# Softmax over a 32768-wide vocabulary: other column pieces for the middle tiles and the last tile

## Chip, cores, metric

One core of one Trainium2 chip. The metric is the time of one execution on the device, in microseconds. The span of a profile is about 1.8 us shorter than the time of the same execution.

## The reference

```python
batch, seq, vocab = 16, 256, 32768          # float32, standard normal draws, temperature 1.0

def reference(logits, temperature):
    scaled = logits / temperature
    scaled = scaled - scaled.max(axis=-1, keepdims=True)
    exp_scaled = np.exp(scaled)
    return (exp_scaled / exp_scaled.sum(axis=-1, keepdims=True)).astype(np.float32)
```

4096 rows of 128 KB are read once and written once: 537 MB each way.

## The kernel before

Each row is cut into two halves on two partitions, so a tile is 128 half-rows of 16384 columns (8.4 MB, 64 KB per partition), and there are 64 tiles in three buffers. Per tile: one load, per column piece a max (DVE) and an exp with that piece's own max (ACT, which also sums), a small chain of statistics that joins pieces and halves, then a scaling shared by DVE and ACT, then one store. A load is issued when the store that last used its buffer has landed.

```python
_SPLIT = 2
_BUFS = 3
_LOAD = 16384
_PIECES = (4096, 4096, 4096, 2048, 2048)     # columns of a piece
_ON_DVE = (4096, 4096, 2048, 0, 0)           # of these, scaled by DVE; ACT scales the rest
_END = 4096                                  # pieces of the first and the last tile
_END_ON_DVE = 2560
# ...
    def store(t, a, b):
        engine = nc.sync if t >= G - 2 else nc.scalar     # SP for the last two tiles, else ACT
        engine.dma_start(out=o[t * P : (t + 1) * P, a:b], in_=buf[t % _BUFS][:, a:b])
# ...
    def normalise(t):
        # ... sizes, on_dve and at: the pieces of this tile
        for k in range(K):
            xc = xs[:, at[k] : at[k] + sizes[k]]
            nc.vector.tensor_reduce(out=nm[:, k : k + 1], in_=xc, axis=X, op=A.max, negate=True)
            # ... (a step for other temperatures, not run here)
            nc.scalar.activation(out=xc, in_=xc, func=Exp, bias=nm[:, k : k + 1],
                                 scale=inv_t, accum_out=ssum[:, k : k + 1])
            if t == 1 and k == 0:
                store(0, 0, W)
        # ... statistics: f[:, k] is the factor of piece k
        for k in range(K):
            a, b, c = at[k], at[k] + on_dve[k], at[k] + sizes[k]
            if b > a:
                nc.vector.tensor_scalar_mul(out=xs[:, a:b], in0=xs[:, a:b], scalar1=f[:, k : k + 1])
            if c > b:
                nc.scalar.activation(out=xs[:, b:c], in_=xs[:, b:c], func=Copy, scale=f[:, k : k + 1])
            if t == G - 1:
                store(t, a, c)               # the last tile is stored piece by piece
        if 0 < t < G - 1:
            store(t, 0, W)

    with tc.manual_schedule():
        for t in range(_BUFS):
            load(t)
        for t in range(G):
            normalise(t)
            if t and t + _BUFS - 1 < G:
                load(t + _BUFS - 1)
```

Of the kernel before, what the change touches and what calls it, by code (L numbers as in the profile page):

```python
# [1 line left out]

# [4 lines left out]


_SPLIT = 2
_BUFS = 3  # L10
_LOAD = 16384
_PIECES = (4096, 4096, 4096, 2048, 2048)
_ON_DVE = (4096, 4096, 2048, 0, 0)
_END = 4096
_END_ON_DVE = 2560
_SETS = 3


@with_exitstack
def kernel(  # L20
    ctx: ExitStack,
    tc: tile.TileContext,
    logits: bass.AP,
    temperature: bass.AP,
    out: bass.AP,
):
    nc = tc.nc
    inv_t = 1.0 / float(temperature)
    P = nc.NUM_PARTITIONS
    fp32 = mybir.dt.float32  # L30
    Exp = mybir.ActivationFunctionType.Exp
    Copy = mybir.ActivationFunctionType.Copy
    X = mybir.AxisListType.X
    A = mybir.AluOpType

    xf = logits.flatten_outer_dims()
    of = out.flatten_outer_dims()
    N, V = xf.shape
    W = V // _SPLIT
    assert sum(_PIECES) == W and len(_PIECES) == len(_ON_DVE)  # L40
    x = xf.rearrange("n (h v) -> (n h) v", h=_SPLIT)
    o = of.rearrange("n (h v) -> (n h) v", h=_SPLIT)
    G = N * _SPLIT // P
    assert G * P == N * _SPLIT
    n_rounds = _SPLIT.bit_length() - 1
    K = max(len(_PIECES), W // _END)

    pool = ctx.enter_context(tc.tile_pool(name="fixed", bufs=1))
    buf = [pool.tile([P, W], fp32, tag=f"x{b}", name=f"x{b}") for b in range(_BUFS)]
    widths = dict(nm=K, ssum=K, ee=K, f=K, ttj=K, nMh=2, Sh=2, rS=1)  # L50
    stat = [
        {
            k: pool.tile([P, w], fp32, tag=f"{k}{s}", name=f"{k}{s}")
            for k, w in widths.items()
        }
        for s in range(_SETS)
    ]

    def load(t: int) -> None:
        n = _END if t in (0, G - 1) else _LOAD  # L60
        for s in range(0, W, n):
            nc.sync.dma_start(  # L62
                out=buf[t % _BUFS][:, s : s + n],
                in_=x[t * P : (t + 1) * P, s : s + n],
            )

    def store(t: int, a: int, b: int) -> None:

        engine = nc.sync if t >= G - 2 else nc.scalar
        engine.dma_start(  # L70
            out=o[t * P : (t + 1) * P, a:b], in_=buf[t % _BUFS][:, a:b]
        )

    def combine(v, op) -> None:
        for j in range(n_rounds):
            mask = [i ^ (1 << j) for i in range(32)]
            nc.vector.stream_shuffle(  # L77
                out=v[:, j + 1 : j + 2], in_=v[:, j : j + 1], mask=mask
            )
            nc.vector.tensor_tensor(  # L80
                out=v[:, j + 1 : j + 2],
                in0=v[:, j : j + 1],
                in1=v[:, j + 1 : j + 2],
                op=op,
            )

    def normalise(t: int) -> None:
        xs = buf[t % _BUFS]
        if t in (0, G - 1):
            sizes = [_END] * (W // _END)  # L90
            on_dve = [_END_ON_DVE] * len(sizes)
        else:
            sizes, on_dve = _PIECES, _ON_DVE
        K = len(sizes)
        at = [sum(sizes[:k]) for k in range(K)]
        st = stat[t % _SETS]
        nm, ssum, ee, f, ttj = (st[k][:, :K] for k in ("nm", "ssum", "ee", "f", "ttj"))
        nMh, Sh, rS = st["nMh"], st["Sh"], st["rS"]
        for k in range(K):
            xc = xs[:, at[k] : at[k] + sizes[k]]  # L100
            nc.vector.tensor_reduce(  # L101
                out=nm[:, k : k + 1], in_=xc, axis=X, op=A.max, negate=True
            )
            if inv_t != 1.0:
                nc.vector.tensor_scalar_mul(
                    out=nm[:, k : k + 1], in0=nm[:, k : k + 1], scalar1=inv_t
                )
            nc.scalar.activation(  # L108
                out=xc,
                in_=xc,  # L110
                func=Exp,
                bias=nm[:, k : k + 1],
                scale=inv_t,
                accum_out=ssum[:, k : k + 1],
            )
            if t == 1 and k == 0:

                store(0, 0, W)
        nc.vector.tensor_reduce(out=nMh[:, 0:1], in_=nm, axis=X, op=A.min)  # L119
        combine(nMh, A.min)  # L120
        nc.scalar.activation(  # L121
            out=ee, in_=nm, func=Exp, bias=nMh[:, n_rounds : n_rounds + 1], scale=-1.0
        )
        nc.vector.tensor_tensor_reduce(  # L124
            out=ttj,
            in0=ee,
            in1=ssum,
            scale=1.0,
            scalar=0.0,
            op0=A.mult,  # L130
            op1=A.add,
            accum_out=Sh[:, 0:1],
        )
        combine(Sh, A.add)
        nc.vector.reciprocal(out=rS, in_=Sh[:, n_rounds : n_rounds + 1])  # L135
        nc.vector.tensor_scalar_mul(out=f, in0=ee, scalar1=rS)  # L136
# [3 lines that stand above are left out]
                nc.vector.tensor_scalar_mul(  # L140
                    out=xs[:, a:b], in0=xs[:, a:b], scalar1=f[:, k : k + 1]
                )
            if c > b:
                nc.scalar.activation(  # L144
                    out=xs[:, b:c], in_=xs[:, b:c], func=Copy, scale=f[:, k : k + 1]
                )
            if t == G - 1:
                store(t, a, c)
# [12 lines that stand above are left out]
# [1 line left out]
_INS = ['logits', 'temperature']  # L162
_OUTS = [((16, 256, 32768), 'float32')]

_NUMBERS = {'temperature': 1.0}


# [26 lines left out]
```

## Time and profile before

| | before |
|---|---|
| time, median of 3 executions | 2496.47 us (2496.07 to 2497.04) |
| span of the profile | 2496.7 us |
| DVE busy, ACT busy | 1575.6 us, 1367.8 us |
| HBM traffic | 430 GB/s over the span |
| DVE waiting for loads | 683.8 us, 66 times |

The page gives busy time per engine, the busy share of 40 equal slices in tenths, and the DMA queues with the share of sixteen DMA engines' span that their packets took. The waits say who waited for whom: total, times, longest. The prediction quotes the lines. To be kept in mind for later: the page counts a DMA engine as busy for the whole duration of a packet, and equal packets do not all take the same time (64 KB took 2418 to 4252 ns in this profile).

### The profile page before, as it was taken

The page shows a single profiled execution, that of the slowest core. Times are in us where ns is not written, and L with a number is a line of the kernel's source. Part 1 is how long each engine was busy: PE and PEld are TensorE (multiplying, and loading weights), DVE is VectorE, ACT ScalarE, POOL GpSimd, SP SyncE. Part 2 cuts the span into 40 slices and gives each one's busy share as a digit, 9 for nine tenths or more (in the row PEclk, how much of TensorE's full clock was granted, in tenths as well). Part 3 has the DMA queues.
Part 4 walks back from the last instruction along what each step waited for, and adds up shares of the span by engine and source line. Part 5 has one row for each costly group of instructions (what it writes and reads, how often), then busy time and mean ns, then how long its engine had stood idle before and what let it go on. Part 6 is the DMA issues. An engine that isn't in the chain of part 4 may idle for free.

```text
span 2496.7 us, 2616 instructions
## 1 busy us (share of the span) xinstructions
DVE 1575.6 (63%) x1216; ACT 1367.8 (55%) x895; POOL 0.2 (0%) x4
## 2 busy tenths in 40 slices
DVE  6576665766657656576565665656657566565665
ACT  6464654645546455464554645546455464554655
POOL 0000000000000000000000000000000000000000
DMA  9999999999999999999999999999999999999998
GB/s 419 436 429 430 433 437 436 435 437 426 434 434 437 433 426 435 434 436 423 433 433 433 435 425 436 436 433 425 435 422 436 421 437 436 421 436 422 436 429 380
DMA packets 19748, 1073.91 MB, mean 430 GB/s; under 512 B 2192, under 2 KB 2192, under 8 KB 2192
## 3 DMA queue, kind: packets, MB, share of 16 engines
q1 hardware_dynamic: 10800, 553.65, 51.4%
q10 hardware_dynamic: 8928, 520.10, 48.4%
q14 instruction: 20, 0.16, 0.0%
HBM read 536.87 MB, written 536.87 MB: 430 GB/s over the span
## 4 chain that ended last, share of the span: by engine, by line
DMA 73%; DVE 16%; ACT 9%; another core or an unknown queue 2%; issue 0%; SPq 0%; DVEq 0%; ACTq 0%
DMA x<-in_logits_dram 37%; DMA out_dram<-x 36%; DVE nm L101 12%; ACT x L108 7%; DVE x L140 3%; ACT x L144 2%; DVE f L136 0%; ACT ee L121 0%; DVE rS L135 0%; DVE Sh L80 0%; DVE ttj L124 0%; DVE Sh L77 0%; SPq L62 0%; DVEq L189 0%
## 5 line engine op out<-in xcount | busy, mean ns | idle before, releaser
L101 DVE TENSOR_REDUCE nm<-x 128x1 f32<-128x4096 f32 x318 | 1117.5, 3579 | 683.8 <-DMA x<-in_logits_dram 683.8
L108 ACT ACTIVATE x<-x,nm 128x4096 f32<-128x4096 f32 x318 | 965.4, 3036 | 1025.3 <-DVE nm L101 1025.3
L144 ACT ACTIVATE x<-x,f 128x2048 f32<-128x2048 f32 (+1 forms) x194 | 370.9, 1975 | 74.0 <-DVE f L136 74.0
L140 DVE TENSOR_SCALAR x<-x,f 128x4096 f32<-128x4096 f32 (+2 forms) x194 | 372.2, 1975 | 2.5 <-DVE f L136 0.2
L124 DVE CUSTOM_DVE_ANT_0 ttj<-ee,ssum 128x5 f32<-128x5 f32 (+1 forms) x64 | 10.6, 166 | 196.7 <-ACT ee L121 196.7
L108 ACT ACTIVATION_READ_ACCUMULATOR x<-x,nm 128x1 f32 x318 | 59.2, 186 | 0.0
L121 ACT ACTIVATE ee<-nm,nMh 128x5 f32<-128x5 f32 (+1 forms) x64 | 18.1, 284 | 0.0
L136 DVE TENSOR_SCALAR f<-ee,rS 128x5 f32<-128x5 f32 (+1 forms) x64 | 14.8, 231 | 2.2
L135 DVE RECIPROCAL rS<-Sh 128x1 f32<-128x1 f32 x64 | 10.5, 164 | 2.2
L80 DVE TENSOR_TENSOR Sh<-Sh 128x1 f32<-128x1 f32 x64 | 10.2, 159 | 2.2
L80 DVE TENSOR_TENSOR nMh<-nMh 128x1 f32<-128x1 f32 x64 | 10.2, 159 | 2.2
L119 DVE TENSOR_REDUCE nMh<-nm 128x1 f32<-128x5 f32 (+1 forms) x64 | 10.1, 158 | 2.2
L77 DVE STREAM_SHUFFLE Sh<-Sh 128x1 f32<-128x1 f32 x64 | 9.7, 151 | 0.0
L77 DVE STREAM_SHUFFLE nMh<-nMh 128x1 f32<-128x1 f32 x64 | 9.7, 151 | 0.0
L108 ACT ACT_TABLE_LOAD x1 | 1.3, 1283 | 8.1 <-DMA x<-in_logits_dram 8.1
L124 DVE DVE_READ_ACCUMULATOR2_ANT Sh<- 128x1 f32 x64 | 5.2, 82 | 0.0
L77 DVE LOAD_MASK_SELECT Sh<-Sh x64 | 0.9, 14 | 2.8
L77 DVE LOAD_MASK_SELECT nMh<-nMh x64 | 0.9, 14 | 2.8
L175 POOL MEMSET const-uint8-127<- 128x1 uint8 x1 | 0.1, 102 | 0.0
L175 POOL MEMSET const-bfloat16-1.0<- 128x1 bf16 x1 | 0.1, 101 | 0.0
L175 POOL MEMSET const-float32-0.0<- 128x1 f32 x1 | 0.1, 98 | 0.2 <-issue 0.2
L175 POOL MEMSET const-float32-1.0<- 128x1 f32 x1 | 0.1, 98 | 0.0
## 6 DMA issues: line engine op xcount, KB each, us to landing
x<-in_logits_dram SPq DMA_DIRECT2D x8, 2048.0 KB, 23.7
out_dram<-x SPq DMA_DIRECT2D x4, 2048.0 KB, 15.1
x<-in_logits_dram SPq DMA_DIRECT2D x62, 43.7
out_dram<-x ACTq DMA_DIRECT2D x62, 44.5
out_dram<-x SPq DMA_DIRECT2D x1, 29.4
```

The source lines that it names most:

```text
L77: nc.vector.stream_shuffle(out=v[:, j + 1 : j + 2], in_=v[:, j : j + 1], mask=mask)
L80: nc.vector.tensor_tensor(out=v[:, j + 1 : j + 2], in0=v[:, j : j + 1], in1=v[:, j + 1 : j + 2], op=op,)
L101: nc.vector.tensor_reduce(out=nm[:, k : k + 1], in_=xc, axis=X, op=A.max, negate=True)
L108: nc.scalar.activation(out=xc, in_=xc, func=Exp, bias=nm[:, k : k + 1], scale=inv_t, accum_out=ssum[:, k : k + 1],)
L119: nc.vector.tensor_reduce(out=nMh[:, 0:1], in_=nm, axis=X, op=A.min)
L121: nc.scalar.activation(out=ee, in_=nm, func=Exp, bias=nMh[:, n_rounds : n_rounds + 1], scale=-1.0)
L124: nc.vector.tensor_tensor_reduce(out=ttj, in0=ee, in1=ssum, scale=1.0, scalar=0.0, op0=A.mult, op1=A.add, accum_out=Sh[:, 0:1],)
L135: nc.vector.reciprocal(out=rS, in_=Sh[:, n_rounds : n_rounds + 1])
L136: nc.vector.tensor_scalar_mul(out=f, in0=ee, scalar1=rS)
L140: nc.vector.tensor_scalar_mul(out=xs[:, a:b], in0=xs[:, a:b], scalar1=f[:, k : k + 1])
L144: nc.scalar.activation(out=xs[:, b:c], in_=xs[:, b:c], func=Copy, scale=f[:, k : k + 1])
L175: nc = _bacc.Bacc("TRN2", target_bir_lowering=False, num_devices=1)
```

## The change

Intent: fewer and longer instructions in the middle tiles (four maxima and exps for five, five scalings for six) at the same split of columns between DVE and ACT, and a shorter tail in the last tile, whose final pieces become smaller. What is moved to and from HBM stays.

```diff
-_LOAD = 16384
-_PIECES = (4096, 4096, 4096, 2048, 2048)
-_ON_DVE = (4096, 4096, 2048, 0, 0)
-_END = 4096
-_END_ON_DVE = 2560
+_LOAD = (16384,)
+_PIECES = (5120, 4608, 4096, 2560)
+_ON_DVE = (5120, 4608, 512, 0)
+_FIRST_PIECES = (4096, 4096, 4096, 4096)
+_FIRST_ON_DVE = (2560, 2560, 2560, 2560)
+_LAST_PIECES = (4096, 4096, 4096, 2048, 2048)
+_LAST_ON_DVE = (2560, 2560, 2560, 2048, 0)
...
+    def cut(t: int) -> tuple:
+        if t == 0:
+            return _FIRST_PIECES, _FIRST_ON_DVE, _FIRST_PIECES
+        if t == G - 1:
+            return _LAST_PIECES, _LAST_ON_DVE, _LAST_PIECES
+        return _PIECES, _ON_DVE, _LOAD
... (load and normalise take their sizes from cut)
```

More of the change, by code (lines that the diff above doesn't have):

```diff
@@ L45 @@
     n_rounds = _SPLIT.bit_length() - 1
-    K = max(len(_PIECES), W // _END)
+    K = max(len(_FIRST_PIECES), len(_PIECES), len(_LAST_PIECES))
     pool = ctx.enter_context(tc.tile_pool(name="fixed", bufs=1))
@@ L57 @@
     ]
+    def cut(t: int) -> tuple:
[4 more added lines that the diff above has]
+        return _PIECES, _ON_DVE, _LOAD
     def load(t: int) -> None:
-        n = _END if t in (0, G - 1) else _LOAD
-        for s in range(0, W, n):
+        s = 0
+        for n in cut(t)[2]:
             nc.sync.dma_start(
@@ L65, in load @@
             )
+            s += n
     def store(t: int, a: int, b: int) -> None:
@@ L88, in normalise @@
         xs = buf[t % _BUFS]
-        if t in (0, G - 1):
-            sizes = [_END] * (W // _END)
-            on_dve = [_END_ON_DVE] * len(sizes)
-        else:
-            sizes, on_dve = _PIECES, _ON_DVE
+        sizes, on_dve, _ = cut(t)
         K = len(sizes)
```

## The prediction

> **What bounds the kernel now.** I read the page from its second part on, because the busy shares of part 1 (DVE 63%, ACT 55%) already say that no compute engine is full. The DMA rows of the 40 slices, the queues and the HBM line come first:
>
> ```profile
> span 2496.7 us, 2616 instructions
> DMA  9999999999999999999999999999999999999998
> q1 hardware_dynamic: 10800, 553.65, 51.4%
> q10 hardware_dynamic: 8928, 520.10, 48.4%
> HBM read 536.87 MB, written 536.87 MB: 430 GB/s over the span
> ```
>
> The reader is to see that the two queues' packets fill 51.4 + 48.4 = 99.8% of 16 DMA engines' span. The kernel reads the input once and writes the output once, so the bytes cannot fall, and the 0.2% left is 5 us: about 2.7 us before the first data arrives and some at the end. Only a change in bytes, in the rate of a packet or in those last microseconds can move the time. The change moves no byte.
>
> Second, the waits, of the engines and then of the issuing queue:
>
> ```profile
> ACT x L108 <- DVE nm L101: 1025.3, 194, 28.4
> DVE nm L101 <- DMA x<-in_logits_dram: 683.8, 66, 24.0
> SPq L62 <- DMA out_dram<-x: 2382.1, 61, 78.9
> ```
>
> DVE waits for a load once per tile, and the loads wait for the store that frees their buffer. ACT's 1025 us behind DVE contain the same wait at one remove. So each tile has slack on the compute side: in the timeline near 1211 us DVE begins a tile when its load lands (1211.78), the store is issued at 1240.10, and the next tile begins at 1250.57. That is a period of about 39 us, with 28.3 us of work and 10.5 us in which DVE waits for DMA.
>
> Third, the end, the only place where data movement and compute are not covered by each other. The timeline of the last stretch and the windows over it:
>
> ```profile
> 2446.73 28.86 SPq L70 DMA_DIRECT2D out_dram<-x  x5
> 2469.14 5.97 ACT L144 ACTIVATE x<-x,f 128x1536 f32<-128x1536 f32 x4 [1.15 <-DVE f L136]
> 2469.26 5.94 DVE L140 TENSOR_SCALAR x<-x,f 128x2560 f32<-128x2560 f32 x4 [0.21 <-DVE f L136]
> 2470.88 4.71 SPq L70 DMA_DIRECT2D out_dram<-x  x4
> ...
> 2466.00:2470.00 4.00, 1.62 (x8) 2.85 (x4) 0.00 (x0) 1.00 0.68 295
> 2470.00:2472.00 2.00, 2.00 (x2) 2.00 (x2) 0.00 (x0) 1.00 0.33 139
> 2472.00:2491.50 19.50, 3.20 (x3) 3.12 (x3) 0.00 (x0) 1.00 0.99 419
> 2491.50:2494.50 3.00, 0.00 (x0) 0.00 (x0) 0.00 (x0) 1.00 0.06 27
> ...
> out_dram<-x SPq DMA_DIRECT2D x1, 29.4
> ```
>
> In a windows line the last two figures are the DMA share and GB/s. Between 2466 and 2472 us most DMA engines have finished the store of tile 62 and wait for the first piece of tile 63: share 0.68, then 0.33. It looks as if earlier compute would pay here. But after 2491.5 us the share is 0.06, 1/16, at 27 GB/s: **one DMA engine of the sixteen** is still moving data. And the store of tile 62, issued at 2446.73, lands only 29.4 us later, at 2476.1, well after the first piece of tile 63 is issued at 2470.88. A transfer lands when its slowest engine is done. The landing records of the single engines say the same: for that store the first came at 2470.1, the fifteenth at 2472.9, the sixteenth at 2476.3; for the last piece 2492.0, 2492.3 and 2495.7. The late engine passes from one store to the next without a gap: 2476.3 plus four pieces of about 4.85 us is 2495.7. So its own backlog, and not the compute of the last tile, sets the end.
>
> **What the Trainium skill says.** "DMA: Bandwidth & Descriptors", section "Where 436 GB/s comes from", puts the ceiling of the sixteen engines at 435.2 GB/s. The trace agrees: 430 GB/s over the whole span, 436 or 437 in the best slices, so nothing in the steady part is left to be won by timing. The same page, section "Issuing engines are not separate DMA queues", says that transfers started by different engines run on the same 16 DMA engines and interleave; here loads come from SP, stores from ACT, and together they are the 430, so the moment at which a store is issued shifts work and adds none. "ScalarE: Activation LUTs", section "What ACT_TABLE_LOAD costs", gives about 280 ns + 0.833 ns per element for an ACTIVATE with a pointer operand. The trace has 1985 ns for 2048 and 3708 ns for 4096 elements, so 0.841 ns per element plus 262 ns: it agrees. "VectorE: DVE Perf Modes", section "The TRN2 errata — SBUF-src ops pay a fixed extra latency per instruction", says that many small instructions pay a fixed term that a large one pays once. The rows by form agree, and show that the term is small against these sizes:
>
> ```profile
> L101 DVE TENSOR_REDUCE nm<-x 128x1 f32<-128x4096 f32 x194 | 845.5, 4413 | 683.8 <-DMA x<-in_logits_dram 683.8
> L108 ACT ACTIVATE x<-x,nm 128x4096 f32<-128x4096 f32 x194 | 719.3, 3708 | 1025.3 <-DVE nm L101 1025.3
> L101 DVE TENSOR_REDUCE nm<-x 128x1 f32<-128x2048 f32 x124 | 277.1, 2276 | 0.0
> L108 ACT ACTIVATE x<-x,nm 128x2048 f32<-128x2048 f32 x124 | 246.1, 1985 | 0.0
> ```
>
> **The change part by part.** All durations below are start-to-start, from the timeline.
>
> *The 62 middle tiles.* Max over five pieces takes 17.46 us now: 4.36 for 4096 columns, 2.19 for 2048. That is 1.0417 us per 1000 columns (17.07 for 16384) plus 0.08 per instruction. With four pieces, 17.07 + 0.32 = 17.39, or 0.07 less on DVE. Exp takes 3.71 and 1.98 with its accumulator read, so 0.845 per 1000 plus 0.25. Now the third exp starts 13.11 us after the tile's start and 3.71 + 1.98 + 1.98 follow: 20.78. After: the max pieces end at 5.42, 10.30, 14.65 and 17.40; exp of the third starts at 14.74 and takes 3.71, the fourth (2560) follows at 18.45 for 2.41: 20.86. So the statistics begin 0.08 later; on four columns they are some 0.01 cheaper. Scaling: DVE has 10240 columns in three instructions before and after, 5.81 us. ACT has 6144 columns, in two instructions instead of three, about 5.79 - 0.2 = 5.6, so DVE ends last. The store is issued at about 28.1 us after the start, where it was 28.06 to 28.3. **Sum: a change of at most 0.1 us per tile, and more likely +0.04**, beside a wait of 10.5 us per tile. On the path that sets the end: 0.
>
> *Tile 0* keeps its pieces. Its store, though, is issued behind the first exp of tile 1, whose first piece grows from 4096 to 5120 columns: 1024 × 1.0417 ns = 1.07 us later, at 47.6 instead of 46.5. At that moment loads of two tiles are in flight or waiting, so the engines stay fed: 0.
>
> *The last tile.* Max 0.07 longer, but the last exp after the third is 1.98 + 1.98 behind the ACT chain: statistics at 13.10 + 3.71 + 1.98 + 1.98 = 20.77 instead of 21.13, 0.36 earlier. Tile 62 frees DVE about 0.06 later, so the first store leaves 0.3 earlier. The last two pieces are scaled on one engine each (about 1.2 and 1.9 us); they are ready about 5.6 and 6.3 us after the scaling starts, where the last one now takes 5.9, but the stores queued ahead need about 20 us. So fifteen DMA engines start 0.3 us sooner, and the sixteenth, with 5 us of tile 62 still before it, does not. On the end: 0, at most -0.3. Two 1 MB transfers replace one of 2 MB, each way: packets of 8192 bytes took 309 ns by the median where 16384 took 611, so 16 of the small ones per engine and direction cost some 0.05 us more in all, with the completion writes of 9 ns.
>
> Sum: 2496.47 + 0 (62 tiles) + 0 (tile 0) + between -0.3 and +0.1 (last tile): **2496.4 us**.
>
> **The rivals.**
> 1. *The round trip of a buffer binds, not the rate.* Load 43.6, work 28.3 and store 44.5 us make 116.4, and three buffers share it: 38.8 per tile, just the period. Then 0.04 more per tile over 62 tiles / 3 buffers, or over every tile, would give +0.8 to +2.5 us, and up to -6 if the work of a tile came out 0.1 shorter. Against it: transfer times of 44 us for 8.4 MB are queueing, since one direction alone moved two tiles in the first 42.04 us, and a queue absorbs a shorter stage. The 99.8% leave no room.
> 2. *The last tile's compute sets the end.* Then its 0.3 us come off in full: 2496.2. For it: share 0.33 in 2470 to 2472. Against it: the one late engine.
> 3. *Another phase of loads and stores changes the rate.* The slices go from 419 to 437 GB/s, and about 13 us per DMA engine lie in packets slower than the common 2418 ns per 64 KB. If the 1 us shift at the start changed which collide, the time could move by 1 or 2 us either way. Nothing speaks for a direction.
>
> **Range and chances.** The three runs of before spread by 1 us. Adding that to rival 1's +2 and rival 2's -0.3, I take **2496.4 us, 2495.0 to 2498.2**. 2% would be 50 us; the DMA floor at 435 GB/s (2468 us, from the skill's figure) excludes faster, and slower would need the work of a tile to grow past its 10.5 us of slack. Chances: faster 0.005, same 0.985, slower 0.01.
>
> **What would show it right or wrong.** Right: DMA share of the queues again 99.8%; DVE waits for loads up by about 0 to 5 us in total; max of a tile 17.4 us; ACT busy lower by about 62 × 2 × 0.26 = 32 us (one exp and one scaling fewer per tile) and DVE by about 62 × 0.14 = 9 us; first store of the last tile 0.3 us earlier but the last landing unchanged. Wrong: a span shorter by over 1 us with the same slow engine would speak for rival 2 or 3; a longer one with DMA gaps, for rival 1.

## The result and the profile after

The changed kernel ran in 2497.36 us by the median of four executions (2494.43, 2495.44, 2499.27, 2504.17), before in 2496.27 us by the median of four (2493.07 to 2497.04). The ratio was 1.0011 with an interval of 0.9987 to 1.0034. A ratio is the mean time of one kernel's runs over that of the other's of the same rounds, so not quite the ratio of the medians. Executions over 1.5% slower than the fastest of the same kernel are left out of the means. The median lies inside the predicted 2495.0 to 2498.2. The mean, 2498.3, does not, nor do three of the four executions, and the predicting median 2496.47 times the ratio is 2499.2. As a statement of where a run of this kernel falls, the range was wrong.

The page of the changed kernel, from an execution of 2494.43 us:

```profile
span 2492.7 us, 2375 instructions
DVE 1571.5 (63%) x1155; ACT 1339.4 (54%) x711; POOL 0.2 (0%) x4
q1 hardware_dynamic: 11088, 553.65, 51.5%
q10 hardware_dynamic: 8928, 520.10, 48.4%
HBM read 536.87 MB, written 536.87 MB: 431 GB/s over the span
```

Compared with before there are 241 instructions fewer, ACT is 28.4 us and DVE 4.1 us less busy, and the two DMA queues again fill the span (99.9%). The waits of the changed kernel:

```profile
DVE nm L107 <- DMA x<-in_logits_dram: 678.8, 66, 22.8
SPq L71 <- DMA out_dram<-x: 2379.2, 61, 78.0
```

The same as before to within 5 us in 2500. One middle tile in the timeline (start, duration, engine, instruction, idle before):

```profile
2338.65 17.40 DVE L107 TENSOR_REDUCE nm<-x 128x1 f32<-128x5120 f32 x4 [11.46 <-DMA x<-in_logits_dram]
2353.36 3.71 ACT L114 ACTIVATE x<-x,nm 128x4096 f32<-128x4096 f32 x1
2359.48 0.28 ACT L127 ACTIVATE ee<-nm,nMh 128x4 f32<-128x4 f32 x1
2360.85 5.81 DVE L146 TENSOR_SCALAR x<-x,f 128x5120 f32<-128x5120 f32 x3
2360.91 5.60 ACT L150 ACTIVATE x<-x,f 128x3584 f32<-128x3584 f32 x2 [1.15 <-DVE f L142]
2366.74 0.34 ACTq L80 DMA_DIRECT2D out_dram<-x  x1
```

The max takes 17.40 us, the statistics start 20.83 us and the store leaves 28.09 us after the tile's start (predicted 17.39, 20.86 and "about 28.1"). So the max, the statistics and the store's moment were priced to a few hundredths of a microsecond, and the change does next to nothing to the store's moment.

What, then, is the difference between an execution of 2494 us and one of 2504? The trace also records every DMA packet with its duration. Most packets of 64 KB take 2418 ns. I add up what each takes beyond that, over 16 engines, and call it the *slow packets*:

```
                span us    slow packets, us per DMA engine    span minus slow
before          2496.7     13.5                               2483.2
changed         2492.7     10.6                               2482.1
```

The profile of the changed kernel is 4.0 us shorter, and 2.9 us of that are packets that were quicker. By the prediction's own signs a span over 1 us shorter with the same late engine would speak for rival 2 or 3. That raised the question the experiments are about: is there an effect of the change at all, and what are slow packets?

### The profile page after: what moved, and what is told of

Same layout as the page of the kernel before. It is cut to its first block, busy times and chain, and to the rows that moved or that the text cites. A ratio compares the mean times of both kernels' runs of the same rounds, so it can differ in the third digit from the quotient of the medians.

```text
span 2492.7 us, 2375 instructions
## 1 busy us (share of the span) xinstructions
DVE 1571.5 (63%) x1155; ACT 1339.4 (54%) x711; POOL 0.2 (0%) x4
## 4 chain that ended last, share of the span: by engine, by line
DMA 73%; DVE 18%; ACT 6%; another core or an unknown queue 2%; issue 1%; SPq 0%; ACTq 0%
DMA x<-in_logits_dram 37%; DMA out_dram<-x 36%; DVE nm L107 13%; ACT x L114 5%; DVE x L146 5%; DVE f L142 0%; ACT x L150 0%; ACT ee L127 0%; DVE rS L141 0%; DVE Sh L90 0%; DVE ttj L130 0%; DVE Sh L87 0%; SPq L71 0%; ACTq L195 0%
## 5 line engine op out<-in xcount | busy, mean ns | idle before, releaser
L107 DVE TENSOR_REDUCE nm<-x 128x1 f32<-128x4096 f32 (+4 forms) x257 | 1113.8, 4395 | 678.8 <-DMA x<-in_logits_dram 678.8
L114 ACT ACTIVATE x<-x,nm 128x4096 f32<-128x4096 f32 (+4 forms) x257 | 948.5, 3691 | 1051.2 <-DVE nm L107 1045.0
L150 ACT ACTIVATE x<-x,f 128x3584 f32<-128x3584 f32 (+2 forms) x132 | 359.7, 2773 | 73.8 <-DVE f L142 73.8
L146 DVE TENSOR_SCALAR x<-x,f 128x5120 f32<-128x5120 f32 (+3 forms) x194 | 371.9, 1973 | 2.3
L130 DVE CUSTOM_DVE_ANT_0 ttj<-ee,ssum 128x4 f32<-128x4 f32 x64 | 10.4, 163 | 202.5 <-ACT ee L127 202.5
L114 ACT ACTIVATION_READ_ACCUMULATOR x<-x,nm 128x1 f32 x257 | 47.9, 186 | 0.0
L127 ACT ACTIVATE ee<-nm,nMh 128x4 f32<-128x4 f32 x64 | 18.0, 282 | 0.0
L142 DVE TENSOR_SCALAR f<-ee,rS 128x4 f32<-128x4 f32 x64 | 14.7, 229 | 2.2
L141 DVE RECIPROCAL rS<-Sh 128x1 f32<-128x1 f32 x64 | 10.5, 164 | 2.2
L90 DVE TENSOR_TENSOR nMh<-nMh 128x1 f32<-128x1 f32 x64 | 10.2, 159 | 2.2
L90 DVE TENSOR_TENSOR Sh<-Sh 128x1 f32<-128x1 f32 x64 | 10.2, 159 | 2.2
L125 DVE TENSOR_REDUCE nMh<-nm 128x1 f32<-128x4 f32 x64 | 10.0, 157 | 2.2
## 6 DMA issues: line engine op xcount, KB each, us to landing
x<-in_logits_dram SPq DMA_DIRECT2D x7, 2048.0 KB, 20.6
```

The costliest lines, as they stand in the source:

```text
L90: nc.vector.tensor_tensor(out=v[:, j + 1 : j + 2], in0=v[:, j : j + 1], in1=v[:, j + 1 : j + 2], op=op,)
L125: nc.vector.tensor_reduce(out=nMh[:, 0:1], in_=nm, axis=X, op=A.min)
L127: nc.scalar.activation(out=ee, in_=nm, func=Exp, bias=nMh[:, n_rounds : n_rounds + 1], scale=-1.0)
L130: nc.vector.tensor_tensor_reduce(out=ttj, in0=ee, in1=ssum, scale=1.0, scalar=0.0, op0=A.mult, op1=A.add, accum_out=Sh[:, 0:1],)
L141: nc.vector.reciprocal(out=rS, in_=Sh[:, n_rounds : n_rounds + 1])
L142: nc.vector.tensor_scalar_mul(out=f, in0=ee, scalar1=rS)
```

## The experiments

Moments of packets and landings below are counted from the span's start, as in the timelines.

**1. Is the difference more than chance?** Four kernels, five rounds each, beside 11 executions of before on the same chip. First, the kernel before timed against itself (no edit):

> The kernel before, unchanged, timed against itself: the size of chance. The four executions of the changed kernel spread over 9.7 us (2494.4 to 2504.2), the four of before over 4.0 us. Theory A (the engines' packet rate differs from execution to execution by some us, whatever the kernel): ratio 1.000 with an interval of about +-0.001 to 0.002, and the single times spread over 5 to 10 us. Theory B (before repeats to 1 us, and the change itself brought the spread and a slower mean): spread of 1 to 4 us, all times 2493 to 2498.

Measured: ratio 0.9983 (0.9961 to 1.0005) for *identical* kernels: six executions from 2493.23 to 2500.31, and eleven from 2494.03 to 2510.28. Theory A holds; before does not repeat to 1 us. The three executions that I predicted from had happened to lie close together.

The changed kernel, no edit:

> The changed kernel, unchanged, for more executions. Theory A (chance): ratio 0.999 to 1.001, mean within 2 us of before's mean of the same rounds. Theory B (the change costs about 0.11 percent): mean 2 to 4 us above before again, ratio 1.001 or more. In the profile: packets slower than the common 2418 ns per 64 KB cost 10 to 14 us per DMA engine, and the span follows that sum by about 1 us per us.

Measured: 0.9989 (0.9964 to 1.0013), six executions from 2493.97 to 2501.37. The sign of the difference turned.

The middle tiles alone (the changed kernel with the last tile of before):

```diff
-_LAST_PIECES = (4096, 4096, 4096, 2048, 2048)
-_LAST_ON_DVE = (2560, 2560, 2560, 2048, 0)
+_LAST_PIECES = (4096, 4096, 4096, 4096)
+_LAST_ON_DVE = (2560, 2560, 2560, 2560)
```

> Only the four pieces of the middle tiles; the last tile as before. Theory A: ratio 1.000 (+-0.001), since 10.5 us of waiting per tile hide the 0.04 us. Theory B with the middle tiles as its cause (round trip of the buffers longer by 0.04 us per tile): +0.8 to +2.5 us.

Measured: 0.9985 (0.9962 to 1.0009).

The last tile alone:

```diff
-_PIECES = (5120, 4608, 4096, 2560)
-_ON_DVE = (5120, 4608, 512, 0)
+_PIECES = (4096, 4096, 4096, 2048, 2048)
+_ON_DVE = (4096, 4096, 2048, 0, 0)
```

> Only the last tile's pieces; the middle tiles as before. Theory A: ratio 1.000. If the last tile's compute sets the end: -0.3 us, not to be told by times. The profile tells: from the landing of the store of tile 62 to the last landing 19.4 to 19.6 us in the slowest engine, as in before (19.35) and in the changed kernel (19.49).

Measured: 0.9991 (0.9966 to 1.0017). From the landing of tile 62's store to the last landing the slowest DMA engine took 19.38 us, where before had 19.35 and 19.15 in two profiles and the changed kernel 19.49 and 19.48.

The changed kernel again, against 11 more executions of before:

> The changed kernel again, for more executions on this chip beside before. Both have the store issued at 28.1 us after the landing, within 0.3 us. If nothing but chance tells them apart: ratio 0.997 to 1.003, both from 2492 to 2510 us.

Measured: 0.9990 (0.9965 to 1.0015). The kernel before has 49 executions with a mean of 2498.8, a median of 2496.6 and a range of 2493.07 to 2525.56 us; the changed kernel has 16 with 2498.1, 2497.9 and 2493.97 to 2504.17. The change does nothing that these runs can see, and it did not bring the spread. (The spread of before itself differed, from 3.7 to 32.3 us.)

In the profiles of this series the span follows the slow packets:

```
               span us   slow packets   span minus slow
aa_before      2494.6    11.5           2483.1
aa_after       2497.9    15.6           2482.3
mid_only       2491.0     8.4           2482.6
last_only      2504.8    22.0           2482.8
aa_after2      2499.7    17.4           2482.3
```

Spans 14 us apart become 0.8 us apart. With equal packets and queues that fill 99.8% of the span this is near to bookkeeping: it says that longer packets, and not idle time, tell these executions apart. It does not say why the packets were longer. (Three profiles of the changed kernel have 2482.1 to 2482.3 and two of before 2483.1 and 2483.2. That may be a real microsecond from the last tile and the middle tiles together; five profiles are too few to call it shown.)

**2. Does the end matter?** Two more maxima in the last tile of before, ahead of its scaling, results unused:

```diff
         nc.vector.tensor_scalar_mul(out=f, in0=ee, scalar1=rS)
+        if t == G - 1:
+            for _ in range(2):
+                nc.vector.tensor_reduce(out=nMh[:, 0:1], in_=xs[:, 0:4096], axis=X, op=A.max)
```

> The last tile alone with two more max before its scaling, 8.7 us. From the issue of tile 62's store to the last landing, and from that store's landing in the slowest engine to the last landing (before: 19.15 to 19.5 us in six profiles). If the slow engine's backlog of about 5.5 us covers part of it: 19.4 becomes about 23 to 25, i.e. +4 to +5. If the last tile's compute sets the end: +8.7, about 28.

Measured in one profile (of a single execution, so its state is unknown): 25.05 us from landing to last landing in the slowest engine, for 19.35 in before. Of 8.7 us, 5.7 reached the end and 3.0 were absorbed. The sixteen engines now finish together (the fifteenth at 2499.76, the last at 2499.78 us), so in this kernel compute sets the end.

The other way, with a wrong result: the last tile is stored as loaded.

```diff
         xs = buf[t % _BUFS]
+        if t == G - 1:
+            for s in range(0, W, _END):
+                store(t, s, s + _END)
+            return
```

> Wrong on purpose: the last tile is stored as it was loaded, with no compute, so that its stores are queued behind tile 62's without a gap. The largest gain that a faster last tile can bring. If the slow engine alone sets the end: from tile 62's landing to the last landing still 19.2 to 19.5 us in the slowest engine, only the fifteen others end earlier. If the last tile's compute counts: up to 1 us less.

Measured, again in one profile of unknown state: 19.44 us. The stores of the last two tiles leave in one go, as the issuing queue shows (before in the first block, this kernel in the second), and the last landing comes no sooner after tile 62's:

```profile
2446.73 28.86 SPq L70 DMA_DIRECT2D out_dram<-x  x5
```

```profile
2444.45 9.58 SPq L70 DMA_DIRECT2D out_dram<-x  x5
```

The five issues took 9.58 us instead of 28.86, for nothing. So in before the late DMA engine sets the end, and nothing in the last tile's compute could have shortened it; the changed kernel's 19.49 us says the same.

**3. Is the wait of 10.5 us per tile slack?** One more max over 4096 columns per middle tile, placed as in experiment 2 with the condition `0 < t < G - 1` and `range(1)`:

> The kernel before, with one more max over 4096 columns (4.36 us on DVE) in each of the 62 middle tiles, put before the scaling, its result unused. If the DMA engines' rate binds and the 10.5 us of waiting per tile are real slack: no change, span minus the loss in slow packets 2483 us as in the six profiles so far (2482.1 to 2483.2), DVE's wait for loads about 62 x 4.36 = 270 us less. If the round trip of a buffer binds (rival 1): each period a third of 4.36 us longer, +90 us, 3.6 percent.

Measured: 2521.53, 2524.93 and 2535.22 us, and 2589.78 in an execution that is left out, called slow because it is 2.7% above the fastest (its granted clock, 1.0, is that of the others, it has no trace, and its cause is unknown); ratio 1.0136 (1.011 to 1.0161). Neither expectation: not 0, not +90, but about +26 to +39 us. The page and waits of its profile:

```profile
span 2519.7 us, 2678 instructions
DVE 1843.6 (73%) x1278; ACT 1367.6 (54%) x895; POOL 0.2 (0%) x4
q1 hardware_dynamic: 10800, 553.65, 51.1%
q10 hardware_dynamic: 8928, 520.10, 48.9%
DVE nm L101 <- DMA x<-in_logits_dram: 440.7, 65, 17.6
```

DVE still waits 440.7 us for loads, 7 us per tile, and DMA still reads 100.0% busy; by both views there is slack and a full DMA, and yet the profiled span is 23 us longer. The slow packets have it: 39.3 us per engine instead of 13.5.

Three such maxima (`range(3)`):

> The same with three more max, 13.1 us per tile, more than the slack of 10.5. If the rate binds up to the slack and then DVE's own serial chain: period 28.1 + 13.1 = 41.2 us instead of 38.8, about +145 us, 5.8 percent, with DVE no longer waiting for loads and DMA share below 0.96. If the round trip binds: 3 times the first run's change, +270 us.

Measured: 2724.97 and 2725.98 us, ratio 1.0918, more than the 41.2 us per tile of DVE's chain explain (+145) and less than the round trip would give. The waits and the queues of its profile:

```profile
DVE nm L101 <- DMA x<-in_logits_dram: 97.3, 27, 10.6
q10 hardware_dynamic: 8928, 520.10, 44.8%
```

The DMA share falls to 95.8%. Past the slack the serial chain binds, and something is added on top: 228 - 145 = 83 us, about 1.3 us per tile. The 97.3 us in which DVE still waited for loads are of that size. Slow packets cost 128.3 us per engine here, the most of all runs; how they lead to these waits was not followed.

**4. What are slow packets?** I went through the packets of each trace against the moments of the stores' issue. After the third store:

```
              all slow   store packets started within   load packets
              packets    5 us after a store's issue     started later
before        12.4       8.0                            3.8
changed        9.4       5.5                            3.5
last_only     20.9       16.0                           4.1
mid_plus1b    38.3       30.9                           6.9
```

(us per DMA engine.) Most of it is in packets opened right after a store's issue. At one tile border of before, the engines' completions of the load came at 1242.8 to 1243.3 us for seven engines, at 1246.5 to 1248.0 for eight and at 1250.5 for the last; the store of the next-to-go tile was issued at 1240.10. Seven engines had finished both of their queued transfers by 1242.9 and opened the new store's first packet, which took 2.8 to 3.6 us instead of 2.4. The next load could not help them, because it waits until the *slowest* engine has landed the earlier store (1245.6). So the reading is: an engine that runs ahead of the others has nothing left at a tile border but the store just issued ("it runs dry"), and this is booked as a longer packet.

The packet records carry this further than one border. Take the first packets of a store that an engine opened right after it had completed its load, and sort them by the time since the store's issue (number of packets, mean ns):

```
              under 2.5 us    2.5 to 3 us    3 to 5 us
before         71, 3180       174, 2796      174, 2424
changed        47, 3050       156, 2754      221, 2418
last_only     158, 3137       350, 2769      193, 2422
mid_plus1b    488, 3174       245, 2809       54, 2418
```

An engine that comes to the store over 3 us after its issue pays next to nothing; one that comes within 2.5 us pays 0.6 to 0.8 us in the mean, and how many come sooner differs between kernels and between executions of one kernel (the changed kernel has 109 and 123 under 2.5 us in its two other profiles). Compute running beside the transfer is no rival for these packets: in before DVE and ACT began nothing for 4.2 us or more after a store's issue (median 10.7). Why a packet opened so early is longer, the trace does not show.

The reading predicts that with no compute between load and store slow packets vanish. Middle tiles stored as loaded:

```diff
         xs = buf[t % _BUFS]
+        if 0 < t < G - 1:
+            if t == 1:
+                store(0, 0, W)
+            store(t, 0, W)
+            return
```

> Wrong on purpose: the 62 middle tiles are stored as they were loaded, with no compute, so that a store is issued as soon as its load has landed. Theory C (slow packets are engines that run dry at a tile boundary because the store of the tile in work is not issued yet): slow packets cost under 2 us per DMA engine, time 2483 to 2486 us, single times within 2 us of each other. Theory A (the rate of packets differs by execution, whatever the kernel): slow packets still 8 to 22 us, 2491 to 2505.

Measured: 2489.83, 2490.57, 2504.12 and 2504.39 us; ratio 0.9996. Its output is wrong, which doesn't matter for the time. In the profile (the execution of 2490.57) slow packets cost 7.3 us, but 193 of the 202 packets over 2450 ns lie in the first 100 us; after that slow packets cost 0.2 us in all. The windows of this kernel (length, busy times, last two figures DMA share and GB/s), then those of before:

```profile
200.00:2440.00 2240.00, 4.86 (x2) 0.81 (x1) 0.00 (x0) 1.00 1.00 434
```

```profile
200.00:2440.00 2240.00, 1421.09 (x1094) 1232.57 (x809) 0.00 (x0) 1.00 1.00 432
```

The DMA share is 1.00 in both; the rates are 434 and 432 GB/s. The Trainium skill's ceiling of 435.2 GB/s ("DMA: Bandwidth & Descriptors", section "Where 436 GB/s comes from") lies 0.3% and 0.7% above these. Theory C holds for the steady part of this profile: without compute between load and store the slow packets are gone. It does not hold for the whole spread, because two of the four executions took 2504 us; they have no trace, and what they lost stays open.

**5. Can the border be mended?** First, the load in two parts, in the changed kernel:

```diff
-_LOAD = (16384,)
+_LOAD = (9728, 6656)
```

> The changed kernel with each middle load cut in two, 9728 and 6656 columns at the border of the second and third piece, so that the max of the first part runs before the second has landed. The store is then issued some 8 to 10 us earlier after the landing. Cost: from 2418 ns per 64 KB and 611 ns per 16 KB packet a fixed 8.7 ns per packet; 8 more packets per engine and tile, 62 tiles: +4.3 us. Theory C: slow packets 0 to 4 us instead of 8 to 22, so in sum 2487 to 2492 us, 5 to 9 us under before, with a spread below 4 us. Theory A: +4 us, spread as before.

Measured: 2606.73 to 2617.28 us, ratio 1.0456 (1.0434 to 1.0478): a miss of 115 us. The store did leave sooner, 17.8 us after the last part had landed in this tile, but the two parts came far apart:

```profile
1186.92 10.35 DVE L107 TENSOR_REDUCE nm<-x 128x1 f32<-128x5120 f32 x2 [11.78 <-DMA x<-in_logits_dram]
1213.88 7.14 DVE L107 TENSOR_REDUCE nm<-x 128x1 f32<-128x4096 f32 x2 [16.62 <-DMA x<-in_logits_dram]
1231.55 17.39 DVE L107 TENSOR_REDUCE nm<-x 128x1 f32<-128x5120 f32 x4
1231.72 0.34 ACTq L80 DMA_DIRECT2D out_dram<-x  x1
```

DVE waits twice in one tile, 28.4 us, and not at all before the next one. Its DMA engines were idle 40 us of the span (before 4), slow packets of 64 KB cost 56 us (before 13.5), and the shorter packets of the load, 1439 and 987 ns when not slow, took another 31 us beyond that. With 4 us for the added packets (these two make 2426 ns for 2418) this is the whole 114 us; so the 8.7 ns per packet were right and the miss lies in idle time and slow packets. Why the pattern is so uneven was not settled.

Second, six falling pieces, so that the store is issued 1.1 us sooner with no change to the transfers:

```diff
-_PIECES = (4096, 4096, 4096, 2048, 2048)
-_ON_DVE = (4096, 4096, 2048, 0, 0)
+_PIECES = (4096, 3456, 2944, 2432, 1920, 1536)
+_ON_DVE = (4096, 3456, 2688, 0, 0, 0)
```

> The kernel before with six falling pieces in the middle tiles (4096, 3456, 2944, 2432, 1920, 1536): the last exp is shorter, so the statistics begin about 1.0 us earlier and the store is issued about 1 us earlier; nothing is added to the transfers. Theory C: from +4.36 us of work costing about +26 us, a slope of some 6 us per us or less on this side: 1 to 6 us faster, slow packets a few us fewer. Theory A: 0.

Measured: 2534.66 to 2541.99 us, ratio 1.0163 (1.0143 to 1.0182): slower by 40 us although less work lies between load and store. The timeline of one tile:

```profile
1230.90 17.52 DVE L101 TENSOR_REDUCE nm<-x 128x1 f32<-128x4096 f32 x6 [12.40 <-DMA x<-in_logits_dram]
1258.13 0.34 ACTq L70 DMA_DIRECT2D out_dram<-x  x1
```

The store leaves 27.23 us after the start, as planned. Slow packets cost 49.0 us. At a border near 1220 us *fourteen* engines had finished both transfers together (landings at 1220.5 to 1221.4) and opened the new store's first packets, 3.2 to 3.5 us each, 1.4 to 2.2 us after its issue, while two engines lagged until 1226 and 1231. In the tally of experiment 4 this kernel has 626 packets under 2.5 us, with a mean of 3223 ns.

Third, was it the moment of the issue? Six pieces with 1.15 us of extra work, ahead of the scaling, and then the old pieces with the earlier moment, wrong (3328 columns unscaled):

```diff
+        if 0 < t < G - 1:                       # six_plus: six pieces, and
+            nc.vector.tensor_reduce(out=nMh[:, 0:1], in_=xs[:, 0:1024], axis=X, op=A.max)
```

> Six pieces with one more max over 1024 columns (1.15 us) ahead of the scaling in the middle tiles, result unused: the store is issued as late as in the kernel before. If the moment of the issue decides (theory D): back to 2492 to 2505 us. If the six pieces cost in another way (more instructions, shorter passes beside the DMA): 2535 to 2545 us, or later.

Measured: 2494.71 to 2498.36 us, ratio 0.9987 (0.9959 to 1.0015). One added instruction of 1.2 us per tile made the six-piece kernel 42 us *faster*.

```diff
             a, b, c = at[k], at[k] + on_dve[k], at[k] + sizes[k]
+            if 0 < t < G - 1 and k == 2:        # minus_2k: five pieces
+                a = b
+                c = b + 768
```

> Wrong on purpose: the kernel before with 3328 columns of the third piece left unscaled in the middle tiles, so that the store is issued about 1.1 us earlier, with the old pieces. Theory D: as six_pieces, 2530 to 2545 us. Otherwise as before or a little faster, 2485 to 2505 us.

Measured: 2493.71 to 2499.31 us, ratio 0.9989 (0.9961 to 1.0018). Its timeline has the same moment as six_pieces, 27.25 us:

```profile
1213.64 17.46 DVE L101 TENSOR_REDUCE nm<-x 128x1 f32<-128x4096 f32 x5 [13.00 <-DMA x<-in_logits_dram]
1240.89 0.34 ACTq L70 DMA_DIRECT2D out_dram<-x  x1
```

So theory D, that the moment of the issue after the tile's start decides, falls: equal moments give 2539 and 2497 us (with before at 2498 and 2497). What differs is how the DMA engines lie to each other, and with it how many reach the new store early (98 packets under 2.5 us in minus_2k, 626 in six_pieces). From the first to the last engine's landing of one transfer:

```
              median us, first to last engine     slow packets, us per engine
before        7.2                                  13.5
changed       7.1                                  10.6
six_plus      7.1                                  13.7
minus_2k      8.8                                  10.3
plus_1k       6.2                                  20.6
six_pieces    4.3                                  49.0
mid_plus1b    3.0                                  39.3
```

Where the engines are staggered over 7 to 9 us, a few at a time run dry and the others are still at work; where they are bunched, nearly all run dry at once. That is a correlation over seven kernels, and a loose one: last_only has 7.7 us and 22.0 us of slow packets, two_loads 7.5 (its stores) and 56, and six_pieces' 4.3 is the median of stores at 3.0 and loads at 10.2. The count of early packets follows the slow packets more closely. Which of these drives the other, and what puts a kernel into one pattern, these runs do not settle.

Last, the old pieces with 1.15 us of extra work (the edit of six_plus on the kernel before):

> The kernel before with one more max over 1024 columns (1.15 us) in the middle tiles. If the cost of longer work is even over the 4.36 us tried: +7 us. If before stands at a favourable moment and both sides fall off as steeply as with six_pieces: +20 to +40 us. If it is flat: 0.

Measured: 2499.45 to 2507.69 us, ratio 1.0016 (0.9986 to 1.0045), slow packets 20.6 us. In the profile the store leaves 29.17 us after the start, 0.8 us later than in a tile of before at the same place. The size fits +7 us, but the interval holds 0 too.

No version here beats before by more than chance. The kernel with no compute in its middle tiles shows how little there is: its two shorter executions, 2490, are 0.3% under before.

## Why the prediction was right or wrong, point by point

- *What the change costs in compute*: right. Max, statistics, ACT's scaling and the store's moment came within 0.05 us. The expected saving on ACT was 32 us of busy time and measured 28.4. On DVE 9 us were expected and 4.1 measured: the 0.14 us per tile contradict the prediction's own sum, 0.07 for the max and three scalings before and after (62 x 0.07 = 4.3). DVE's waits for loads were to rise by 0 to 5 us and fell by 5.0.
- *No effect on the time from the middle tiles, and the verdict "same"*: right by the three timings (middle alone, last alone, both: all within the scatter of before against itself). In part this was luck: the prediction took small shifts of compute to be harmless, and six_pieces, also a mere cut into other pieces, cost 40 us.
- *The late DMA engine sets the end, so the last tile's 0.3 us do not count*: right, and experiment 2 speaks against rival 2, with one profile each way. Relative to the issue of tile 62's store, the first store of tile 63 was issued 0.50 us earlier (23.66 for 24.16 us; 0.3 predicted) and its first landing came 0.48 us earlier (29.81 for 30.29 us); the slow engine's stretch did not shrink (19.49 for 19.35). The "5 us" of backlog was too much: 3.0 us were absorbed. (The single engines' landings that the prediction quotes, 2470.1 to 2495.7, are 0.24 us late against its own timeline, where tile 62's store lands at 2476.1; their differences are right.)
- *The range*: wrong, and this is the step that failed: "The three runs of before spread by 1 us. Adding that to rival 1's +2 and rival 2's -0.3". Three executions were taken for the scatter of the kernel; the term for chance was mis-sized. The scatter of before, over 49, has a standard deviation of 6.0 us and single times up to 2525.56. A range of 3.2 us could not hold the mean of four executions reliably, even with the right centre: of the sixteen executions of the changed kernel 6 lie within 2495.0 to 2498.2, and of the 49 of before 21. What the profiles show behind the scatter is slow packets, 8.4 to 22.0 us per engine from one execution to the next; what sets their number in an execution stays open.
- *"The 99.8% leave no room"*: wrong as a reading. Inside that share lay 13.5 us per engine of packets that took longer than 2418 ns. The prediction saw them, as rival 3 ("about 13 us per DMA engine lie in packets slower than the common 2418 ns"), but gave the rival 1 or 2 us either way. There were 8.4 to 22.0 us of slow packets in seven profiles of before, the changed kernel and their halves, and 49 in a kernel whose store moved by 1.1 us. Rival 3 named the right place, mis-sized; but that this change acted through it is not shown, since executions of one kernel differ as much (10.6 to 17.4 us in three profiles of the changed kernel).
- *"the moment at which a store is issued shifts work and adds none"*: wrong. Six pieces issued the store 1.1 us sooner and took 2539 us; one more max of 1.2 us in the same kernel brought 2497.
- *"beside a wait of 10.5 us per tile"*: the wait is not slack in full. 4.36 us of it, used, cost 26 to 39 us. The change used 0.04 us of it, and no cost was seen.

## What to carry to other kernels

Time a kernel against itself before you believe a difference, or predict a range, below half a per cent: three close executions prove no repeatability. A DMA queue that reads 100% busy may hold packets that take longer than they need; count how long equal packets take, and look at the borders between transfers, where an engine that runs ahead finds only a store that has just been issued. Here the time answered to small shifts of compute in both directions and not in proportion, so a shift has to be tried, and tried again.

## What the Trainium skill lacked or had wrong

- No page says how long equal packets can differ at a full DMA share (it would belong to "DMA: Bandwidth & Descriptors"). Here 64 KB packets took 2418 ns, and 3.0 to 3.2 us in the mean when they were the first of a store and opened within 2.5 us of its issue by an engine that had just completed its load; together 8 to 49 us per engine and run at a share of 99.8 to 100%.
- The same page, section "Latency and other measured facts", calls some DMA engines usually slower and gives a guess that is tied to transfers issued from GpSimd. Here all transfers were issued from SP and ACT, and still one of sixteen engines landed 2.7 us (median of before) after the fifteenth. But its last packets took 611 ns per 16 KB like the others', and the lag was 0.7 us in mid_plus1b and 0.1 in mid_raw: these runs show an engine that is behind, not one that is slower, and the trace does not say which it was.
- The same section's 0.6 us to the first byte agrees: in before the first packet of the first load opened 1.02 us after its issue began and 0.64 us after the issuing instruction ended.
- No page says what a second part of a load costs: from 2418 ns for 64 KB and 611 ns for 16 KB a fixed 8.7 ns per packet can be worked out, but two parts per load cost 115 us per run, not the 4.3 us of that sum. The rest was some 36 us more idle time and 74 us more of slow packets, whose cause is not explained here.
